# The first pair of gate and up: computed from h block by block instead of by seven products, with the factors of h on VectorE alone

## The chip, the cores and the metric

One core of a Trainium2 chip runs the whole program. The time is device microseconds of one launch: before, 2615.62 us as the median of three runs (2615.2 to 2616.56). A profiled execution of the same program took 2614.02 us, of which 2612.3 us lie between its first and its last instruction (its span).

## What is computed

The reference is one layer of a hybrid decoder for 1024 prompt tokens and 64 sample tokens (8 groups of 8), so 1088 token columns, with a model width of 1024. The layer is a half feed-forward, an attention and Mamba mixer with an output projection, a second half feed-forward and a final norm. The change is in the two feed-forwards:

```python
def rmsnorm(x, w):
    xf = x.astype(jnp.float32)
    y = xf * lax.rsqrt(jnp.mean(xf * xf, axis=-1, keepdims=True) + EPS)
    return (y * w.astype(jnp.float32)).astype(x.dtype)

def ffn_half(x, nw, wg, wu, wd):
    h = rmsnorm(x, nw)
    return x + 0.5 * ((jax.nn.silu(h @ wg) * (h @ wu)) @ wd)
```

wg and wu are 1024 x 2816: 22 blocks of 128 feature rows, handled as 11 pairs.

## The kernel before

**Number format.** All products are float32 in value. Each operand is split into a high part, rounded to the TensorE format fp32r, and a low part, the rest (`split`: a cast on ScalarE, VectorE or GpSimd, and a subtraction). A product then takes three matmuls: high x high, low x high, high x low.

**Seven products.** h, transposed, stands as eight blocks of 128 model features by 1088 tokens. It is seen as a 2 x 2 matrix: features 0 to 511 (blocks kk = 0..3) and 512 to 1023 (blocks kk + 4), by token half (544 columns each): h11, h21 are the two feature halves of the first token half, h12, h22 those of the second. A pair of 128-row blocks of a weight, with its two feature halves, is a 2 x 2 matrix too. The 2 x 2 product is made by seven products instead of eight (Winograd's form). It needs seven factors B1..B7 of h (h11, h21, h22, h12-h11, h22-h12 and two longer sums) and seven factors of each weight pair, every one as a high and a low tile. The factors of h are made once per feed-forward (`b_make`) and used by 11 pairs of gate and 11 of up; the factors of a weight (`factors`) are made for each pair. The token halves are worked in two column parts, `SUBS`: 256 columns (part 0), then 288 (part 1) of each half. A product is 4 x 3 matmuls (k = 0..3) with a moving operand of 256 or 288 columns, so one pair of one weight has 7 x 12 x 2 = 168 of them, and `Product.product` then adds each into the result tile `Cc` on ScalarE or VectorE (lines 358 to 372).

**The first pair (p = 0) of a feed-forward** runs while the factors of h come into being, since nothing else can run then. In the first feed-forward `x_sub(z)` makes part z of h: sums of squares on ScalarE (`x_rms`, line 591), transposes on TensorE into PSUM (line 607), the normed value h on VectorE (line 609), a copy of the raw value to DRAM by ScalarE (line 610), and `b_make` for each block kk. `begin1` then orders: seven products of gate on part 0, part 1 of h, seven of up on part 0, and, with the weight factors made a second time, gate and up on part 1. In the second feed-forward `begin2` does the same; part 0 of its factors (`b0`) is made between the output projection's last products (`out`, lines 1877 to 1886), and part 1 after the norm of the layer's x (`x2_sq`, `x2_rms`, `h_row`). Which engine does each subtraction and cast of these first factors is written in the strings CFG1, CFG2 and BC: v is VectorE, p GpSimd, a ScalarE.

```python
CFG1 = [('pvppvppvppv', 'vvvvavv'), ('pvppvvvppvv', 'aaaaaaa'), ...
BC = [('vvpvvppvppv', 'vvvvvvv'), ('pvpvvppvvpv', 'vvaaaaa'), ...
```

**Pairs p = 1..10** use `Product` with subtractions on VectorE and casts on ScalarE. While pair p runs, `g_factors` splits the result of pair p - 1 for the down projection and writes it to DRAM (GD).

**What sets the order.** The program is written once; a scheduler that estimates the time of each instruction lays it out as one fixed queue per engine, and a queue waits at its first instruction that is not ready. Tiles come from pools: a new tile of a tag waits for one of the tag's buffers to come free (for `Cc` three, for the PSUM tags X and Y four banks each).

Of the kernel before, what the change touches and what calls it, by code (L numbers as in the profile page):

```python
# [82 lines left out]
def hybrid_step(ctx: ExitStack, tc: tile.TileContext, *aps):  # L83
# [34 lines left out]
    F1X, F1R, F1, F1W, F1T = (F1s.enter_context(pool(nm, bufs=2)) for nm in ("f1x", "f1r", "f1c", "f1w", "f1t"))  # L118
# [7 lines left out]
    for tag, bufs in (("h0", 2), ("h1", 2), ("h2", 1), ("h3", 1), ("t0", 1), ("t1", 1), ("xRs", 2)):  # L126
        FX.first(tag, [P, 288], bufs)
# [22 lines left out]
    raw0 = F1R.tile([P, 8, 2 * P], F32, name="raw", tag="raw", bufs=2)  # L150
# [1978 lines left out]
```

## Time and profile before

| quantity | before |
|---|---|
| median of the runs | 2615.62 us |
| profiled execution, its span | 2614.02 us, 2612.3 us |
| TensorE (PE) busy | 2465.2 us, 94% of the span |
| VectorE (DVE) busy | 1863.4 us, 71% |
| ScalarE (ACT) busy | 1103.0 us, 42% |
| GpSimd (POOL) busy | 642.9 us, 25% |
| last up result of pair 0, first feed-forward | added at 120.81 us |
| last up result of pair 0, second feed-forward | added at 1938.72 us |

Rows of the timeline read: start, length, engine, line, operation, result<-operands, shape, and in brackets how long the engine was idle before and who ended it. Instructions overlap at their ends by some 0.07 us on VectorE and by more on TensorE, so the time that one takes from its queue is read from start to start. Rows of windows read: busy time (and count) of PE, PE's weight loads, DVE, ACT and POOL, the granted PE clock, the share of the DMA engines, GB/s.

### The profile page before, as it was taken

The numbers are of one execution on the slowest core, as the hardware profiler recorded it, in microseconds if no ns is written. First come the engines' busy times: TensorE is split into PE (matmuls) and PEld (weight loads), VectorE is DVE, ScalarE is ACT, GpSimd is POOL, SyncE is SP. The second block draws the span as 40 slices with busy tenths as digits, with TensorE's granted clock in tenths as the row PEclk, the third lists the DMA queues.
The fourth block names the chain that finished last, engine by engine and source line by source line (L and its number), as shares of the span: only waits on it lengthen the run. The fifth ranks groups of instructions, "written<-read, shape, count | busy, mean of one in ns | idle before, by whom it ended". The sixth has DMA issues, their size and how long they took to land.

```text
span 2612.3 us, 47418 instructions
## 1 busy us (share of the span) xinstructions
PE 2465.2 (94%) x18647; PEld 2291.2 (88%) x18647; DVE 1863.4 (71%) x3699; ACT 1103.0 (42%) x2410; POOL 642.9 (25%) x703
## 2 busy tenths in 40 slices
PE   5899999999999999999999979999689999999998
PEld 4799999999999999878787756678689999999998
DVE  7967676776677556377778877567986766768666
ACT  4544444431233223277777633423244544442113
POOL 5500000013234223444344345232620000002220
PEclk9899999999999999999999989989889999999999
DMA  4243443496553222220101134352123434469653
GB/s 138 83 164 134 149 153 127 167 385 256 198 193 104 88 60 90 89 82 33 65 34 36 54 130 162 120 180 95 54 99 123 164 128 160 150 230 349 234 185 146
DMA packets 209531, 365.05 MB, mean 140 GB/s; under 512 B 17053, under 2 KB 130377, under 8 KB 207388
## 3 DMA queue, kind: packets, MB, share of 16 engines
q1 hardware_dynamic: 190376, 305.10, 33.6%
q0 software_dynamic: 7600, 38.59, 4.1%
q10 hardware_dynamic: 11332, 18.33, 2.0%
q8 instruction: 147, 2.41, 0.4%
q14 instruction: 76, 0.62, 0.1%
HBM read 246.39 MB, written 119.71 MB: 140 GB/s over the span
## 4 chain that ended last, share of the span: by engine, by line
PE 45%; DVE 9%; DMA 3%; ACT 2%; issue 1%; POOL 0%; SPq 0%; DVEq 0%; ACTq 0%; POOLq 0%
PE gY L353 3%; PE gY L352 3%; PE gY L354 3%; PE dq L551 3%; PE dq L552 3%; PE dq L553 3%; PE gX L353 2%; PE gX L354 2%; PE gX L352 2%; PE pT L1521 2%; PE o L1526 1%; PE o L1527 1%; PE s L1484 1%; PE cA L1397 1%; PE s_ps L1743 1%
## 5 line engine op out<-in xcount | busy, mean ns | idle before, releaser
L552 PE MATMUL dq<-db,da 128*128 128x256 f32 (+1 forms) x1232 | 354.7, 290 | 3.1 <-DVE da L258 2.9
L553 PE MATMUL dq<-db,da 128*128 128x256 f32 (+1 forms) x1232 | 354.2, 289 | 0.0
L551 PE MATMUL dq<-db,da 128*128 128x256 f32 (+1 forms) x1232 | 349.2, 290 | 5.1 <-DMA db<-GD 3.3
L557 DVE TENSOR_TENSOR xT<-xT,dq 128x256 f32<-128x256 f32 (+1 forms) x520 | 210.1, 431 | 118.5 <-PE dq L553 117.3
L258 POOL TENSOR_TENSOR ds<-dw 128x512 f32<-128x512 f32 x22 | 29.1, 1323 | 1033.3 <-PE gY L353 423.1
L552 PEld LDWEIGHTS dq<-db,da 128*128 128x128 f32 x1232 | 233.4, 190 | 4.5 <-DVE da L258 4.3
L551 PEld LDWEIGHTS dq<-db,da 128*128 128x128 f32 x1232 | 230.4, 190 | 6.5 <-ACT da L255 2.4
L553 PEld LDWEIGHTS dq<-db,da 128*128 128x128 f32 x1232 | 234.0, 190 | 0.0
L255 ACT CAST whi<-ws 128x512 fp32r<-128x512 f32 x178 | 110.4, 623 | 219.0 <-PE gY L354 155.5
L255 ACT CAST da<-ds 128x512 fp32r<-128x512 f32 x88 | 51.9, 619 | 254.0 <-PE dq L553 91.5
L258 DVE TENSOR_TENSOR wlo<-raw,whi 128x512 fp32r<-128x512 f32 x149 | 109.0, 737 | 70.3 <-ACT whi L255 69.9
L258 DVE TENSOR_TENSOR wlo<-ws,whi 128x512 fp32r<-128x512 f32 x175 | 124.6, 715 | 47.3 <-ACT whi L255 46.5
L255 ACT CAST whi<-raw 128x512 fp32r<-128x512 f32 x158 | 98.0, 626 | 77.3 <-DMA raw<-in_w_out_dram 49.0
L1500 ACT ACTIVATE pb<-s,mx 128x256 f32<-128x256 f32 (+3 forms) x192 | 105.4, 555 | 36.0 <-DVE mx L1498 17.2
L258 DVE TENSOR_TENSOR pl<-pT,ph 128x512 fp32r<-128x512 f32 (+1 forms) x148 | 100.1, 683 | 20.8 <-ACT ph L255 19.5
L352 PE MATMUL gY<-B3h,whi 128*128 128x256 f32 (+1 forms) x352 | 101.8, 290 | 6.1 <-DVE Cc L368 5.4
L353 PE MATMUL gY<-B5h,wlo 128*128 128x256 f32 (+1 forms) x352 | 101.9, 290 | 4.8 <-DVE wlo L258 4.7
L352 PE MATMUL gX<-B6h,whi 128*128 128x256 f32 (+1 forms) x352 | 103.5, 294 | 2.8 <-ACT Cc L359 2.5
L353 PE MATMUL gY<-B4h,wlo 128*128 128x256 f32 (+1 forms) x352 | 101.9, 292 | 3.7 <-DVE wlo L258 3.7
L352 PE MATMUL gY<-B4h,whi 128*128 128x256 f32 (+1 forms) x352 | 99.8, 291 | 5.2 <-DVE whi L255 3.2
L255 ACT CAST ph<-pT 128x512 fp32r<-128x512 f32 (+1 forms) x148 | 84.8, 588 | 46.4 <-PE pT L1521 44.4
L352 PE MATMUL gX<-B1h,whi 128*128 128x256 f32 (+1 forms) x352 | 100.8, 293 | 3.2 <-DVE whi L255 2.4
(683 smaller groups left out, 8853.3 us busy)
## 6 DMA issues: line engine op xcount, KB each, us to landing
db<-GD SPq DMA_DIRECT2D x42, 1632.0 KB
GD<-Cc SPq DMA_DIRECT2D x154, 272.0 KB
GD<-his SPq DMA_DIRECT2D x84, 272.0 KB
raw<-in_ffn_wg_dram SPq DMA_DIRECT2D x22, 1024.0 KB
raw<-in_ffn_wu_dram SPq DMA_DIRECT2D x22, 1024.0 KB
dw<-in_ffn_wd_dram SPq DMA_DIRECT2D x44, 512.0 KB
GD<-hp SPq DMA_DIRECT2D x70, 272.0 KB
db<-GD SPq DMA_DIRECT2D x14, 1088.0 KB
```

Of the source, the lines that this page charges most:

```text
L255: nc.scalar.copy(out, src) if eng == "a" else ENGINES[eng].tensor_copy(out, src)
L258: ENGINES[eng].tensor_tensor(out, x, y, op=op)
L352: nc.tensor.matmul(q, ah[:, k], b_, start=first, stop=False, skip_group_check=True)
L353: nc.tensor.matmul(q, al[:, k], b_, start=False, stop=False, skip_group_check=True)
L354: nc.tensor.matmul(q, ah[:, k], c_, start=False, stop=(k == 3), skip_group_check=True)
L551: nc.tensor.matmul(q, x, bh[:, u, o], start=first, stop=False, skip_group_check=True)
L552: nc.tensor.matmul(q, y, bh[:, u, o], start=False, stop=False, skip_group_check=True)
L553: nc.tensor.matmul(q, x, bl[:, u, o], start=False, stop=(u == np_ - 1), skip_group_check=True)
L557: nc.vector.tensor_tensor(x, x, q, op=OP.subtract if i == 4 else OP.add)
L1397: nc.tensor.matmul(ab, wh, mh, start=first, stop=False, skip_group_check=True)
L1500: nc.scalar.activation(pb[:, st:st + pn], s, AF.Exp, bias=mx[:, 0:1], accum_out=part[:, hh_, i:i + 1])
L1521: nc.tensor.transpose(tq_[:kn, P * hh_:P * hh_ + P], src, ident)
```

## The change

For p = 0 alone the seven products are replaced by the plain eight. Class `First` takes the four blocks of h as they are (B1 = h11, B4 = h12 for now, B2 = h21, B3 = h22) and two feature blocks of the raw weight (kk and kk + 4, 256 columns), splits them in one 128 x 512 piece, and accumulates all of a column part in PSUM: per kk 2 x 2 x 2 x 3 = 24 matmuls, as soon as block kk of h is there. Gate leaves PSUM through SiLU on ScalarE, up through one multiplication on VectorE (`silu_out`, `times_out`); the additions into `Cc` and the sums of weight blocks fall away for this pair. `b_make` first splits the four plain blocks, then makes the differences; the sum that belongs in B4 is kept in a tile T4, and `b_last` writes it over h12 once First has read it. All subtractions of these factors are on VectorE, all casts on ScalarE; CFG1, CFG2 and BC are gone. In the second feed-forward T4 and three of the h rows take two of the three `Cc` buffers for a while, and "hp" has five buffers instead of four.

```diff
-    def b_make(K, h, kk, z, eng="vvpvvppvppv", heng="vvaaaaa"):
+    def b_make(z, kk, h):
...
         def put(i, src):
-            split(BN[z][i][0][:, kk], BN[z][i][1][:, kk], src, next(e), next(he))
+            split(BN[z][i][0][:, kk], BN[z][i][1][:, kk], src, "v")
         put(1, h11)
         put(2, h21)
...
+        put(4, h12)
+        put(3, h22)
+        sub("v", h11, h12, h11)
+        sub("v", h12, h22, h12)
+        sub("v", h22, h22, h11)
+        sub("v", t4, h22, h21)
+        put(6, h22)
         put(7, h12)
-        put(5, t1)
-        put(3, h22)
-        sub(next(e), h21, t2, h21)
-        put(4, h21)
+        put(5, h11)
+
+    def b_last(z):
+        for kk in (0, 2):
+            split(*(t[:, kk:kk + 2] for t in (*BN[z][4], T4[z])), "v")
...
+    class First:
...
+        def run(self, z, kk, bank):
+            c0, n = SUBS[z]
+            src = self.raw[:, kk::4]
+            hi, lo = (F1W.tile([P, 2, 2 * P], F32R, name=f"w{c}", tag=f"w{c}", bufs=4) for c in ("hi", "lo"))
+            split(hi, lo, src, "v")
+            if kk == 0:
+                if z == 0:
+                    t = [bank("g0") for _ in range(2)]
+                    self.q = {(f, j): t[f][:, n * j:n * j + n] for f in range(2) for j in range(2)}
+                else:
+                    self.q = {(f, j): bank("g0")[:, :n] for f in range(2) for j in range(2)}
+            for i in range(2):
+                for j in range(2):
+                    bh, bl = (t[:, kk] for t in BN[z][((1, 4), (2, 3))[i][j]])
+                    for f in range(2):
...
+                        nc.tensor.matmul(q, hi[:, i, o], bh, start=first, stop=False, skip_group_check=True)
+                        nc.tensor.matmul(q, lo[:, i, o], bh, start=False, stop=False, skip_group_check=True)
+                        nc.tensor.matmul(q, hi[:, i, o], bl, start=False, stop=last, skip_group_check=True)
+            if kk == 3:
+                for f in range(2):
+                    for j in range(2):
+                        self.out(self, f, slice(HALF * j + c0, HALF * j + c0 + n), self.q[f, j])
+
+    def silu_out(g, f, o, q):
+        nc.scalar.activation(g.C[:, f, o], q, AF.Silu)
...
-    def begin1(g, u):
-        for i in ORDER:
-            g.product(i, 0)
-        x_sub(1)
-        for i in ORDER:
-            u.product(i, 0)
-        for x, c in ((g, CFG1[2]), (u, CFG1[3])):
-            x.begin(*c)
-            for i in ORDER:
-                x.product(i, 1)
+    def begin1():
+        g = First(F1, w1g, silu_out, raw0)
+        x_sub(0, lambda kk: g.run(0, kk, bankx))
+        u = First(F1, w1u, times_out(g))
+        for kk in range(4):
+            u.run(0, kk, bankx)
+        x_sub(1, lambda kk: g.run(1, kk, bankx))
+        b_last(0)
+        for kk in range(4):
+            u.run(1, kk, banky)
+        b_last(1)
+        return [g, u]
```

**Place 1: VectorE in the first feed-forward, a block of part 1.** Names: h_* are normed blocks, B1h/B1l the high and low tile of factor 1, t_* differences, ws sums of weight blocks, wlo low parts of weights. Before, VectorE's queue has there:

```order
L609 SCALAR_TENSOR_TENSOR h_643<-x_ps,w_170,xRs 128x288
L609 SCALAR_TENSOR_TENSOR h_650<-x_ps,w_170,xRs 128x288
L258 TENSOR_TENSOR B3l_77<-h_614,B3h_76 128x288
L258 TENSOR_TENSOR wlo<-ws_851,whi 128x512
L258 TENSOR_TENSOR B5l_84<-t_618,B5h_83 128x288
L255 CAST B1h_111<-h_643 128x288
L370 TENSOR_TENSOR Cc<-Cc,gY 128x256
L258 TENSOR_TENSOR B6l_98<-t_619,B6h_97 128x288
```

and GpSimd's beside it, before:

```order
L258 TENSOR_TENSOR h_598<-t_619,h_598 128x288
L258 TENSOR_TENSOR B7l_91<-h_607,B7h_90 128x288
L258 TENSOR_TENSOR ws_889<-raw,ws_831 128x512
L258 TENSOR_TENSOR wlo<-ws_830,whi 128x512
L258 TENSOR_TENSOR B1l_112<-h_643,B1h_111 128x288
L258 TENSOR_TENSOR t_670<-h_659,h_643 128x288
```

Now VectorE has:

```order
L641 SCALAR_TENSOR_TENSOR h_771<-x_ps,w_168,xRs 128x288
L257 TENSOR_TENSOR B4l_70<-h_705,B4h_69 128x288
L641 SCALAR_TENSOR_TENSOR h_778<-x_ps,w_168,xRs 128x288
L257 TENSOR_TENSOR B3l_77<-h_712,B3h_76 128x288
L257 TENSOR_TENSOR h_705<-h_712,h_705 128x288
L257 TENSOR_TENSOR B5l_84<-h_689,B5h_83 128x288
L257 TENSOR_TENSOR B1l_112<-h_771,B1h_111 128x288
L257 TENSOR_TENSOR h_712<-h_712,h_689 128x288
L257 TENSOR_TENSOR B2l_105<-h_778,B2h_104 128x288
```

GpSimd's queue has no instruction in this feed-forward's first pair any more; VectorE has all subtractions, no casts, and no sums of weights.

**Place 2: TensorE in the first feed-forward, the change from part 0 to part 1.** Before, the transposes of part 1 (x_ps) stand in the middle of the products of part 0:

```order
L354 MATMUL gX<-B6l_96,whi 128x256
L352 MATMUL gY<-B4h_67,whi 128x256
L607 MATMUL x_ps<-ident,xt 128x128 x2
L607 MATMUL x_ps<-ident,xrest 128x32
L607 MATMUL x_ps<-ident,xt 128x128 x2
L607 MATMUL x_ps<-ident,xrest 128x32
L352 MATMUL gX<-B7h_88,whi 128x256
```

Now (g_519 and g_520 are up's sums on part 0; xR spreads the norm of part 1):

```order
L398 MATMUL g_520<-B3h_74,wlo 128x256
L399 MATMUL g_520<-B3l_75,whi 128x256
L216 MATMUL xR<-ident,xr_634 128x128 x2
L216 MATMUL xR<-ident,xr_634 128x32
L216 MATMUL xR<-ident,xr_659 128x128
L216 MATMUL xR<-ident,xr_659 128x96
L216 MATMUL xR<-ident,xr_659 128x64
L639 MATMUL x_ps<-ident,xt 128x128 x2
L639 MATMUL x_ps<-ident,xrest 128x32
```

The norm and the transposes of part 1 moved behind all of gate's and up's products on part 0.

**Place 3: the second feed-forward.** Before, TensorE has products of gate on part 0 between the two steps of part 1's norm (nps sums, nR spreads):

```order
L354 MATMUL gY<-B2l_20727,whi 128x256
L743 MATMUL nps<-ones,acc 128x1 x4
L743 MATMUL nps<-ones,acc 64x1
L352 MATMUL gY<-B5h_20741,whi 128x256
L353 MATMUL gY<-B5h_20741,wlo 128x256
L354 MATMUL gY<-B5l_20742,whi 128x256
```

Now all of them stand behind the norm:

```order
L239 MATMUL wout<-ol,whi 128x288
L781 MATMUL nps<-ones,acc 128x1 x4
L781 MATMUL nps<-ones,acc 64x1
L216 MATMUL nR<-ident,nr 128x128 x4
L791 MATMUL nps<-ident,nr 128x64
L397 MATMUL g_21456<-B1h_20663,whi 128x256
```

And VectorE now has, at the end of the factors of part 1 (hpc: h rows in a `Cc` buffer; g_21649 and g_21650: up's sums on part 0; L410 is `times_out`):

```order
L257 TENSOR_TENSOR T_20704<-hpc 128x288
L257 TENSOR_TENSOR B6l_21422<-hpc,B6h_21421 128x288
L257 TENSOR_TENSOR wlo<-raw,whi 128x512
L410 SCALAR_TENSOR_TENSOR Cc<-Cc,g_21649 128x256 x2
L410 SCALAR_TENSOR_TENSOR Cc<-Cc,g_21650 128x256 x2
L257 TENSOR_TENSOR ws_22097<-raw 128x512
L257 TENSOR_TENSOR ws_22141<-raw 128x512
L257 TENSOR_TENSOR ws_22098<-ws_22097,raw 128x512
L257 TENSOR_TENSOR wlo<-raw,whi 128x512 x5
```

`times_out` of part 0 stands behind the last use of hpc, and frees the PSUM banks that gate's second half of part 1 takes; the first sums of the next pair's weight (ws) stand ahead of the low parts of up's weight for part 1 (wlo).

More of the change, by code (lines that the diff above doesn't have):

```diff
@@ L149, in hybrid_step @@
         x_load(t0, n)
-    raw0 = F1R.tile([P, 8, 2 * P], F32, name="raw", tag="raw", bufs=2)
+    raw0 = f32(F1R.tile([P, 8, 2 * P], F32R, name="raw", tag="raw", bufs=2))
     nc.sync.dma_start(raw0, A["ffn1_wg"][0][:, :2 * P].rearrange("(k p) f -> p k f", p=P))
@@ L429, in gate_up @@
                         up(int(i == 4))
-            elif p == 0:
-                ps.append(Product(K, wu, p, 1, cfg=cfg[1]))
-                begin(*ps)
-                for f in range(2):
-                    gate(f)
-                    up(f)
-            else:
+            elif p:
                 for x in every:
@@ L455, in gate_up @@
             pass
-    raws, loaded = {}, []
+    loaded = []
     def gu_raw(K, w, p):
-        raw = F1R.tile([P, 8, 2 * P], F32, name="raw", tag="raw", bufs=2)
+        raw = f32(F1R.tile([P, 8, 2 * P], F32R, name="raw", tag="raw", bufs=2))
         load = nc.sync.dma_start(raw, w[:, 2 * P * p:2 * P * p + 2 * P].rearrange("(k p) f -> p k f", p=P))
@@ L622, in x_sub @@
             x_block(s, kk)
+            product(kk)
     def late():
@@ L1920, in hybrid_step @@
     FX = Ahead(F1X)
-    FX.first("hp", [P, 576], 4)
-    for tag in ("t0", "t1"):
-        FX.first(tag, [P, 288])
+    FX.first("hp", [P, 576], 5)
     FX.first("acc", [P, 576], 2)
@@ L1958, in h_row, with h_of @@
         return h
+    def h_of(x, y):
+        n = x.shape[-1] // 2
+        return x[:, :n], y[:, :n], x[:, n:], y[:, n:]
+    t4 = F1.tile([P, 4, HALF], F32, name="T4", tag="Cc", bufs=3)
+    T4[0], T4[1] = t4[:, :, :256], t4[:, :, 256:]
     for m in range(KD):
@@ L1977, in hybrid_step @@
     x2_rms(1)
[L1978 to L1981 removed]
+    hp = [FX.tile("hp", [P, 576], 5) for _ in range(5)]
+    c = F1.tile([P, 2, T], F32, name="hpc", tag="Cc", bufs=3).rearrange("p a t -> p (a t)")
+    hp += [c[:, 576 * u:576 * u + 576] for u in range(3)]
     rows = {m: h_row(m, 1, hp.pop(0)) for kk in range(4) for m in (kk, kk + 4)}
@@ L1996, in banky, with begin2 @@
         return PY.tile([P, 512], F32, name=name, tag="Y", bufs=4)
-    def begin2(g, u):
-        for i in ORDER:
-            g.product(i, 0)
+    def begin2():
+        g = First(F1, A["ffn2_wg"][0], silu_out)
         for kk in range(4):
-            b_make(FX, h_of(rows[kk], rows[kk + 4]), kk, 1, *BC[3])
-        for i in ORDER:
-            u.product(i, 0)
-        for x, c in ((g, CFG2[2]), (u, CFG2[3])):
-            x.begin(*c)
-            for i in ORDER:
-                x.product(i, 1)
-    gate_up(F1, A["ffn2_wg"][0], A["ffn2_wu"][0], begin2, CFG2, lambda: FX.tile("hp", [P, HALF], 4, F32R),
-            lambda: [FX.tile("hp", [P, 4, P], 4) for _ in range(3)])
+            g.run(0, kk, bankx)
+        for kk in range(4):
+            b_make(1, kk, h_of(rows[kk], rows[kk + 4]))
+        u = First(F1, A["ffn2_wu"][0], times_out(g))
+        for kk in range(4):
+            u.run(0, kk, bankx)
+        b_last(0)
+        for kk in range(4):
+            g.run(1, kk, bankx)
+        for kk in range(4):
+            u.run(1, kk, banky)
+        b_last(1)
+        return [g, u]
+    gate_up(F1, A["ffn2_wg"][0], A["ffn2_wu"][0], begin2(), lambda: FX.tile("hp", [P, HALF], 5, F32R),
+            lambda: [FX.tile("hp", [P, 4, P], 5) for _ in range(3)])
     R2s.close()
```

75 lines of the change are left out of this document (35 added, 40 removed).

## The prediction

> **What bounds the kernel now.** I read the page's span, then the busy time of each engine in stretches of the two feed-forwards, then the timeline's rows in them, and the groups by shape.
>
> ```profile
> span 2612.3 us, 47418 instructions
> ```
>
> The windows give start:end, length, then the busy time (and count) of TensorE (PE), its weight loads, VectorE (DVE), ScalarE (ACT), GpSimd (POOL), the granted clock, the DMA share and GB/s:
>
> ```profile
> 11.00:56.00 45.00, 24.98 (x97) 19.78 (x98) 43.70 (x88) 16.84 (x53) 29.72 (x30) 0.94 0.37 120
> 56.00:118.40 62.40, 52.62 (x332) 46.43 (x332) 56.26 (x92) 32.41 (x74) 37.67 (x32) 0.85 0.20 62
> 118.40:140.00 21.60, 21.60 (x175) 21.60 (x174) 19.09 (x33) 12.00 (x23) 0.00 (x0) 1.00 0.67 230
> ...
> 1811.00:1860.00 49.00, 41.50 (x288) 39.08 (x286) 48.30 (x78) 13.65 (x28) 35.20 (x33) 0.97 0.27 85
> 1860.00:1902.00 42.00, 24.38 (x140) 22.16 (x140) 38.51 (x59) 13.25 (x32) 23.66 (x21) 0.74 0.08 27
> 1902.00:1936.00 34.00, 30.47 (x203) 29.16 (x204) 27.64 (x42) 15.74 (x30) 12.37 (x9) 0.87 0.15 46
> 1936.00:2100.00 164.00, 164.00 (x1329) 164.00 (x1328) 118.06 (x203) 77.90 (x155) 0.00 (x0) 1.00 0.45 151
> ```
>
> From 118.4 and from 1936 on PE has no gap: 21.60 of 21.60 us and 164.00 of 164.00. In the first pair of the first feed-forward (11 to 118.4) it has 77.6 of 107.4 us, while DVE has 100.0 and POOL 67.4; in the second (1811 to 1936) PE has 96.4 of 125, DVE 114.5. So **DVE's list of factors bounds the first pairs, PE all that follows**, and what a first pair gains passes to the end 1:1. Its end on PE:
>
> ```profile
> 118.56 0.38 ACT L359 COPY Cc<-gX 128x256 f32<-128x256 f32 x1 [0.92 <-PE gX L354]
> ...
> 120.81 0.46 DVE L370 TENSOR_TENSOR Cc<-Cc,gY 128x288 f32<-128x288 f32 x1 [1.24 <-PE gY L354]
> ...
> 1938.72 0.46 DVE L370 TENSOR_TENSOR Cc<-Cc,gY 128x288 f32<-128x288 f32 x1 [1.25 <-PE gY L354]
> ```
>
> DVE adds up's last product of pair 0 at 120.81; at 118.56 a product of pair 1 was already copied out, so by the queue some 18 matmuls had run ahead: 18 x 0.13 = 2.3 us, and the pair's work equals an end at 118.4. In the same way 1938.72 stands for 1936.3.
>
> DVE's busy time is stretched. Two groups of one shape, the one beside POOL, the other mostly without it:
>
> ```profile
> L258 DVE TENSOR_TENSOR B6l<-t,B6h 128x288 fp32r<-128x288 f32 x4 | 4.3, 1066 | 0.0
> ...
> L258 DVE TENSOR_TENSOR t<-h,t 128x288 f32<-128x288 f32 x4 | 1.8, 448 | 0.0
> ```
>
> 1066 ns against 448. The rows that stand alone, read from start to start:
>
> ```profile
> 19.52 0.41 DVE L258 TENSOR_TENSOR B1l<-h,B1h 128x256 fp32r<-128x256 f32 x1
> 19.85 0.41 DVE L258 TENSOR_TENSOR B2l<-h,B2h 128x256 fp32r<-128x256 f32 x1
> ...
> 70.90 1.35 DVE L609 SCALAR_TENSOR_TENSOR h<-x_ps,w,xRs 128x288 f32<-128x288 f32 x3
> ...
> 115.13 0.68 DVE L258 TENSOR_TENSOR ws<-raw 128x512 f32<-128x512 f32 x1
> 115.73 0.68 DVE L258 TENSOR_TENSOR wlo<-raw,whi 128x512 fp32r<-128x512 f32 x1
> ...
> 1905.13 0.45 DVE L258 TENSOR_TENSOR B5l<-t,B5h 128x288 fp32r<-128x288 f32 x1
> 1905.50 0.44 DVE L258 TENSOR_TENSOR hpc<-t,hpc 128x288 f32<-128x288 f32 x1
> ```
>
> **Prices.** A subtraction of 256 columns goes by 0.33 (19.52 to 19.85), of 288 by 0.37, of 512 by 0.60; three h rows of 288 by 0.43 each. The h row of 256, read from PSUM, I put between those at 0.39, a 576-wide one at 0.65. PE and ACT:
>
> ```profile
> 20.93 0.41 PE L352 MATMUL gX<-B1h,whi 128*128 128x256 f32 x1
> 21.14 0.41 PE L353 MATMUL gX<-B1h,wlo 128*128 128x256 f32 x1
> ...
> 39.14 0.58 PE L352 MATMUL gX<-B1h,whi 128*128 128x256 f32 x1 [0.40 <-DVE B1h L255]
> ...
> 47.00 0.30 PE L353 MATMUL gY<-B5h,wlo 128*128 128x256 f32 x1
> ...
> 62.39 0.28 PE L354 MATMUL gX<-B1l,whi 128*128 128x256 f32 x1
> 62.50 0.28 PE L352 MATMUL gX<-B1h,whi 128*128 128x256 f32 x1
> ...
> 63.18 0.38 PE L607 MATMUL x_ps<-ident,xt 128*128 128x128 f32 x2
> ...
> 63.67 0.44 PE L607 MATMUL x_ps<-ident,xt 128*128 128x128 f32 x2
> ...
> 115.63 0.29 PE L352 MATMUL gY<-B4h,whi 128*128 128x288 f32 x1
> 115.76 0.30 PE L353 MATMUL gY<-B4h,wlo 128*128 128x288 f32 x1
> ```
>
> ```profile
> 18.65 0.58 ACT L591 ACTIVATE xsq<-xt 128x512 f32<-128x512 f32 x1
> ...
> 65.41 0.45 ACT L255 CAST B7h<-h 128x288 fp32r<-128x288 f32 x1
> ...
> 105.70 1.28 ACT L413 ACT_TABLE_LOAD   x1
> ...
> L413 ACT ACTIVATE Cc<-Cc x44: 1097/1111/1117, 107.0 to 2353.2; 128x1088 f32<-128x1088 f32 x44
> ```
>
> A matmul of 256 columns has a pitch of 0.115 (62.39, 62.50) or, at half rate, 0.21 (20.93, 21.14); of 288 it has 0.13 (115.63). After an idle stretch PE worked from 39.14 to about 47.00 at the slow pitch before the fast one came, 7.8 us, so a cold start costs some 3.5 us.
>
> The Trainium skill ("TensorE: Matmul & The Clock Gate", Part 1 on the clock gate) says that the array runs at half clock for about 3.4 us of activity and falls back after an idle window. The two pitches agree, the 7.8 us do not; by the page's 3.4 each cold start would cost about 1.7 us, an estimate, and the sum below would be some 5 us lower.
>
> **What goes and what comes.** The plain eight need 4 x 24 = 96 matmuls per weight and column part, 384 per feed-forward, where seven products needed 336: 48 more, 48 x 0.123 = 5.9 us of PE. Gone are the first pair's additions into Cc, the sums of weight blocks, the second making of weight factors, and all of POOL's part. DVE's list in the first feed-forward is now 16 h rows and 4 outputs of up (L609-like, one operand in PSUM) of each width, 44 subtractions of each width, 16 weight low parts and 2 pieces of B4 of 512, 2 of 576: 20 x 0.39 + 20 x 0.43 + 44 x 0.33 + 44 x 0.37 + 18 x 0.60 + 2 x 0.65 + 1 = **60 us** where 100.0 were busy. If the stretch were not POOL's, the same list at 0.8 to 1.0 an instruction would take some 100 us and nothing would be won on DVE. ACT gets all casts: 56 of h (0.34, row 65.41) and 20 of weights or B4 (0.6, as the 512-wide square), 32 raw copies (0.37), 20 squares (0.6, row 18.65) and 8 SiLUs, about 58 us. SiLU from PSUM is in no row; the nearest below is the copy Cc<-gX, 0.38, above it a whole SiLU of 1088 columns (1.11 for the last row's group); I take 0.4, near the copy, whose width it has. At 1.11 the eight would cost ACT 6 us more ahead of part 1. Up's outputs lie between the 0.37 and 0.46 of rows above. The table loads for SiLU and the root cost 1.28 each (105.70).
>
> **First feed-forward.** The first h row stood at 14.30, that of part 1 at 55.78:
>
> ```profile
> 14.30 0.86 DVE L609 SCALAR_TENSOR_TENSOR h<-x_ps,w,xRs 128x256 f32<-128x256 f32 x2
> ...
> 55.78 0.93 DVE L609 SCALAR_TENSOR_TENSOR h<-x_ps,w,xRs 128x288 f32<-128x288 f32 x2
> ```
>
> Now four gate low parts (4 x 0.60) precede h: start at 16. Part 0 then needs of DVE 16 x 0.39 + 44 x 0.33 + 4 x 0.60 = 23.2, to about 40; of PE 192 x 0.115 = 22, transposes 5 (16 groups without the remainder), a cold start 3.5, and it is fed block by block: I put its end at 50 (bounds 46.5, the bare sum from 16, and 58, a wait of 3 for each of four blocks). The norm of part 1 moves behind part 0 on PE (transposes) and behind SiLU on ACT (queue order): from gate's end near 44, two table loads 2.6, SiLUs 1.6, ten squares 6, root, spread and copies 2: first h at 57, PE idle about 5. Part 1 from there: PE 192 x 0.13 = 25, transposes 8.6 (16 groups of 0.49, rows 63.18 and 63.67, and the spread of the norm), cold start 3.5, so 37; DVE 16 x 0.43 + 44 x 0.37 + 8 x 0.60 = 28 lies beside it. End 94, with 2 for waits **96, a gain of 22** from 118.4. Bounds: 88.6 when the handover costs 4 instead of 7 and neither start is cold (gain 30), 105 when part 0 ends at 58 (gain 13).
>
> **Second feed-forward.**
>
> ```profile
> 1859.49 0.44 DVE L1886 TENSOR_TENSOR xT<-xT,wout 128x288 f32<-128x288 f32 x1
> ...
> 1867.64 3.86 DVE L1956 SCALAR_TENSOR_TENSOR hp<-xT,vec,acc 128x576 f32<-128x576 f32 x4 [0.84 <-ACT acc L755]
> ...
> 1921.36 0.37 SPq L461 DMA_DIRECT2D raw<-in_ffn_wg_dram  x1
> ...
> 1929.95 1.74 DVE L258 TENSOR_TENSOR ws<-raw 128x512 f32<-128x512 f32 x1
> ```
>
> The output projection's last add is at 1859.49; there PE was idle 7.5 of 49 us while DVE (48.30 of 49) made part 0's factors with POOL's 35.2 beside it. The new DVE list in this stretch is 16 x 0.39 + 44 x 0.33 for factors and about 16 for the projection, 37: end at 1852 (bounds 1848, PE without idle and 4 more for what it also shed, and 1860, nothing won). The norm takes 8.15 from there to the h rows (1859.49 to 1867.64) and gate's products now stand behind it: 1858 + 22 + 3.5 = 1883.5. Meanwhile DVE does the 8 h rows of 576 (0.74, twice 0.37; at most 0.97, 3.86 / 4), 44 x 0.37, 8 x 0.60 and 1.2 of B4: from 1860 to 1888.5. Only then come up's outputs, since u.C waits for the tile of the h rows; the PSUM banks of gate's part 1 wait for them, so **a new wait of about 5 us** stands on PE ahead of gate's second half, with all of gate and up part 1 behind it: 1889 + 192 x 0.13 = **1914, a gain of 22** from 1936.3. The next pair's ws<-raw stands ahead of five low parts on DVE; its load went out at 1921.36 and its tile was read by 1929.95, so at most 8.6 us; issued now near 1886.5 it lands by 1895, needed at 1899: covered by some 4 us, beyond which each microsecond late costs one. Bounds: 1901 (projection 1848, no cold start, half the wait), gain 35; 1926 (projection 1860, the rest as above, 4 more wait), gain 10.
>
> **Sum.** 22 + 22 = 44. The profiled execution took 2614.0 us, the median of the runs 1.6 more: 2615.6 - 44 = **2571.5 us**. The bounds (23 to 65) give 2550 to 2592.
>
> **Rivals.**
> 1. *Half pitch in the block-by-block parts.* PE is fed in pieces there, and rows 20.93 to 47.00 show half pitch under such feeding; against it, gaps become shorter than before. Part 0 at 192 x 0.21 = 40 instead of 22 + 3.5: the first pair ends near 111, the second's at 1928, gains 7 and 8: 2600. The skill's rule on the clock (same page and part) falls in with this if every window has idle time.
> 2. *The handovers of the queues swallow half.* DVE, ACT and PE each hold some 60 us in order; against it, ACT was the least busy of the three (16.84 of 45 and 32.41 of 62.40 us), so its new load has room. If only one feed-forward gains, 2615.6 - 22 = 2593.
> 3. *Better.* No cold start and no wait at the handovers: 2550.
> 4. *Slower.* PE stays at half pitch in both column parts of both feed-forwards: 192 x (0.21 + 0.24) = 86 us of matmuls per feed-forward. First: 16 + 40 + 4 to 60, 7 of handover, 46 and transposes at half pitch to 134 (loses 16); second: 1858 + 40 + 46 and the wait of 5 to 1949 (loses 13): 2644. It decides once more than 44 / 0.11 = 400 of the 768 matmuls run so. Against it: rows 62.39 to 62.50 already have the full pitch in part 1 before.
> 5. *It does not do what it says*: the stretch of DVE stays though POOL is idle, and PE's 2 x 5.9 us come on top: 2627. Row pairs such as 1066 against 448 speak against it.
>
> **How the numbers follow.** Forecast 0.62, rival 1 0.10, rival 2 0.14, rival 3 0.06, rival 4 0.05, rival 5 0.03. The range takes the forecast's bounds, widened to most of rivals 1 to 3: 2546 to 2602; the likeliest case by itself has 2550 to 2592. This measurement tells 0.2%, some 5 us, from no change. Faster: 0.62 + 0.10 + 0.14 + 0.06 less 0.01 for their edges, 0.91; within 0.2%: 0.02; slower 0.07.
>
> **What would show it.** Right: DVE's subtractions of 256 and 288 columns at means of 0.41 and 0.45 with POOL empty in 11 to 100; first h of part 1 at 57; the pair's end at 96; in the second feed-forward an idle PE of some 5 us ahead of gate's second half, ended by up's output; from the pairs' ends on a PE without gaps. Wrong: a pitch of 0.21 in most of part 0, DVE means near 0.8, or PE idle in the later pairs (a load or factor late there), which would cost beside all of this.

## The result, and the profile after

| quantity | before | after |
|---|---|---|
| median of the runs | 2616.09 us (4 runs, 2615.2 to 2616.96) | 2573.79 us (4 runs, 2572.59 to 2577.71) |
| ratio of the medians, 95% interval | | 0.9841, 0.9824 to 0.9858 |
| profiled execution, its span | 2614.02, 2612.3 us | 2574.34, 2572.6 us |
| GpSimd busy | 642.9 us | 508.1 us |
| VectorE busy | 1863.4 us | 1781.9 us |

The changed kernel is 42.3 us faster by the medians, 39.7 by the profiled executions; the forecast was 2571.5. The stretches of the changed kernel, in the form of the windows of before (start:end, length, then busy us and count of PE, its weight loads, DVE, ACT, POOL, then the granted clock, DMA share, GB/s):

```profile
11.00:50.00 39.00, 32.39 (x234) 30.50 (x234) 30.16 (x79) 31.06 (x89) 0.00 (x0) 1.00 0.43 138
50.00:57.00 7.00, 2.84 (x11) 2.18 (x11) 2.03 (x6) 4.13 (x9) 0.00 (x0) 0.62 0.44 148
57.00:96.00 39.00, 38.58 (x221) 33.07 (x220) 30.09 (x74) 22.19 (x56) 0.00 (x0) 0.81 0.27 84
...
1811.00:1850.00 39.00, 34.62 (x236) 33.65 (x235) 33.18 (x69) 18.84 (x42) 4.09 (x3) 0.87 0.40 130
1850.00:1875.00 25.00, 25.00 (x208) 25.00 (x207) 23.41 (x58) 15.56 (x37) 0.00 (x0) 1.00 0.07 21
1875.00:1900.00 25.00, 25.00 (x195) 25.00 (x194) 14.82 (x26) 10.54 (x19) 0.00 (x0) 1.00 0.27 89
...
1936.00:2100.00 164.00, 164.00 (x1331) 164.00 (x1330) 117.29 (x203) 76.84 (x155) 0.00 (x0) 1.00 0.43 148
```

POOL is empty in the first pair of the first feed-forward, DVE went from 100.0 busy us to about 63, and PE's largest hole is at 50 to 57. In the windows from 1850 on PE has no gap. The trace has no record of the clock ahead of its first change (20.99 here), and the windows print 1.00 there. The groups of VectorE's subtractions in 11 to 98 (last columns: busy us, mean ns of one, idle before):

```profile
L257 DVE TENSOR_TENSOR h<-h,h 128x288 f32<-128x288 f32 x12 | 5.4, 453 | 0.0
L257 DVE TENSOR_TENSOR h<-h,h 128x256 f32<-128x256 f32 x12 | 5.0, 420 | 0.1
L257 DVE TENSOR_TENSOR B6l<-h,B6h 128x288 fp32r<-128x288 f32 x4 | 1.8, 453 | 0.0
```

The low part of B6, which took 1066 ns beside POOL, takes 453. The marks on which the working stood, in the timeline after (in brackets how long the engine had been idle, and who ended it):

```profile
16.58 1.80 DVE L641 SCALAR_TENSOR_TENSOR h<-x_ps,w,xRs 128x256 f32<-128x256 f32 x4 [1.74 <-PE x_ps L639]
...
54.16 1.75 PE L216 MATMUL xR<-ident,xr 128*128 128x128 f32 x6 [4.54 <-DVE xr L214]
...
56.81 0.52 DVE L641 SCALAR_TENSOR_TENSOR h<-x_ps,w,xRs 128x288 f32<-128x288 f32 x1 [2.80 <-PE x_ps L639]
...
98.31 0.28 PE L351 MATMUL gX<-B1h,whi 128*128 128x256 f32 x1
...
1834.88 0.45 DVE L1924 TENSOR_TENSOR xT<-xT,wout 128x288 f32<-128x288 f32 x1
...
1843.69 0.58 PE L397 MATMUL g<-B1h,whi 128*128 128x256 f32 x1
...
1868.08 0.30 PE L398 MATMUL g<-B1h,wlo 128*128 128x288 f32 x1
...
1872.01 1.40 DVE L410 SCALAR_TENSOR_TENSOR Cc<-Cc,g 128x256 f32<-128x256 f32 x4
...
1874.32 0.29 PE L397 MATMUL g<-B4h,whi 128*128 128x288 f32 x1
...
1893.42 0.28 PE L351 MATMUL gX<-B1h,whi 128*128 128x256 f32 x1
```

The pairs p = 1 begin on PE at 98.31 and 1893.42, where before the equivalents were 118.4 and 1936.3. So the first feed-forward gained 20.1, and up to the second pair's end the program gained 42.9. The difference, 22.8, is not what the second feed-forward gained, for the lead of the first did not arrive there whole. Three like rows, first before, then after (the same SiLU of a later pair in each feed-forward, and between them the reciprocal in the norm that is taken during the output projection):

```profile
182.13 1.11 ACT L413 ACTIVATE Cc<-Cc 128x1088 f32<-128x1088 f32 x1
1806.34 0.18 DVE L215 RECIPROCAL nr<-nr 128x4 f32<-128x4 f32 x1 [0.27 <-ACT nr L214]
1999.62 1.11 ACT L413 ACTIVATE Cc<-Cc 128x1088 f32<-128x1088 f32 x1
```

```profile
162.84 1.11 ACT L452 ACTIVATE Cc<-Cc 128x1088 f32<-128x1088 f32 x1
1793.05 0.18 DVE L214 RECIPROCAL nr<-nr 128x4 f32<-128x4 f32 x1 [0.27 <-ACT nr L213]
1956.71 1.11 ACT L452 ACTIVATE Cc<-Cc 128x1088 f32<-128x1088 f32 x1
```

The lead is 19.3 us at the first, 13.3 at the second and 42.9 at the third: 6.0 us were lost between the feed-forwards, and the second one gained 29.6. Most of the loss lies from 1715 to 1775, where PE has the output projection among its work and waits for a weight's high part, 1.51 us before and 4.53 after:

```profile
1765.81 0.49 PE L238 MATMUL wout<-oh,whi 128*128 128x512 f32 x1 [1.51 <-ACT whi L255]
```

```profile
1751.61 0.79 PE L237 MATMUL wout<-oh,whi 128*128 128x512 f32 x1 [4.53 <-ACT whi L254]
```

In that stretch PE, DVE, ACT and POOL have the same instructions in the same order before and after, but for one matmul. The loss mostly goes with the time that the clock is at half between the first pair's end and 1790: 81.9 us before, 92.2 after. Of the runs below, three with 99.0 us there lost 8.4 of their lead on the way (the two mixed ones and the order of loads alone), two with 81.9 lost 1.2 and 1.6, and one with 75.1 (the third that fills the hole) lost nothing; but the early norm lost only 2.8 with 92.2. What causes the loss is not shown.

From the second pair's end to the end of the span it took 2572.6 - 1893.4 = 679.2 instead of 676.0: **3.2 us were given back**, at a place that the prediction had not looked at. 19.3 - 6.0 + 29.6 - 3.2 is the 39.7 of the profiled executions. The rows of TensorE's waits in the last 280 us, before and after (total us, times, longest):

```profile
PE dq L551 <- DMA db<-GD: 2.1, 1, 2.1
```

```profile
PE dq L584 <- DMA db<-GD: 8.5, 3, 4.9
```

It is the last down projection, whose products wait for their operands (db). SyncE's queue there, before and after (SPq: the issue of DMAs):

```profile
2335.11 5.74 SPq L698 DMA_DIRECT2D xT<-xD  x2
2342.22 7.88 SPq L504 DMA_DIRECT2D db<-GD  x3
```

```profile
2297.10 0.38 SPq L537 DMA_DIRECT2D db<-GD  x1
2297.53 0.93 SPq L736 DMA_DIRECT2D xT<-xD  x2
2300.17 4.56 SPq L537 DMA_DIRECT2D db<-GD  x2
```

The scheduler laid this queue in another order, though nothing of the change is there: one db now stands ahead of the two loads of x and holds them. Down's first product started at 2355.47 before, 20 us behind the first issue of x, and at 2310.09 after, 12.6 us behind it.

### The profile page after: what moved, and what is told of

Same layout as the page of the kernel before. It is cut to its first block, busy times and chain, and to the rows that moved or that the text cites. A ratio compares the mean times of both kernels' runs of the same rounds, so it can differ in the third digit from the quotient of the medians.

```text
span 2572.6 us, 47482 instructions
## 1 busy us (share of the span) xinstructions
PE 2459.7 (96%) x18743; PEld 2293.1 (89%) x18743; DVE 1781.9 (69%) x3677; ACT 1114.6 (43%) x2452; POOL 508.1 (20%) x581
## 4 chain that ended last, share of the span: by engine, by line
PE 46%; DVE 6%; DMA 4%; ACT 2%; issue 2%; POOL 1%; SPq 0%; DVEq 0%; ACTq 0%; POOLq 0%
PE gY L352 3%; PE gY L351 3%; PE gY L353 3%; PE dq L584 3%; PE dq L586 3%; PE dq L585 3%; PE gX L351 2%; PE gX L352 2%; PE gX L353 2%; PE pT L1559 2%; DMA db<-GD 1%; PE o L1565 1%; PE o L1564 1%; PE s L1522 1%; DMA chk<-in_cache_cmp_dram,idx 1%
## 5 line engine op out<-in xcount | busy, mean ns | idle before, releaser
L254 ACT CAST whi<-ws 128x512 fp32r<-128x512 f32 x156 | 96.4, 622 | 210.7 <-PE gY L353 142.2
L254 ACT CAST whi<-raw 128x512 fp32r<-128x512 f32 x176 | 108.9, 625 | 91.2 <-DMA raw<-in_w_out_dram 48.3
L257 DVE TENSOR_TENSOR wlo<-ws,whi 128x512 fp32r<-128x512 f32 x156 | 106.9, 689 | 41.5 <-ACT whi L254 41.0
L1535 DVE TENSOR_REDUCE mx<-s 128x1 f32<-128x384 f32 (+2 forms) x128 | 67.5, 536 | 38.6 <-PE s L1527 30.2
L264 POOL TENSOR_TENSOR pb<-pb,sm 128x640 f32<-128x640 f32 (+7 forms) x70 | 84.9, 1236 | 44.1 <-DVE sm L1545 43.6
L351 PE MATMUL gY<-B3h,whi 128*128 128x256 f32 (+1 forms) x320 | 91.5, 287 | 1.4 <-ACT whi L254 1.4
L352 PE MATMUL gX<-B6h,wlo 128*128 128x256 f32 (+1 forms) x320 | 91.8, 287 | 0.5 <-DVE wlo L257 0.5
L351 PE MATMUL gX<-B6h,whi 128*128 128x256 f32 (+1 forms) x320 | 91.4, 286 | 0.7 <-ACT Cc L358 0.7
L352 PE MATMUL gY<-B3h,wlo 128*128 128x256 f32 (+1 forms) x320 | 91.7, 287 | 0.2 <-DVE wlo L257 0.2
```

The source lines that it names most:

```text
L254: nc.scalar.copy(out, src) if eng == "a" else ENGINES[eng].tensor_copy(out, src)
L257: ENGINES[eng].tensor_tensor(out, x, y, op=op)
L264: nc.gpsimd.tensor_tensor(out, x, by.to_broadcast(list(x.shape)), op=OP.mult)
L351: nc.tensor.matmul(q, ah[:, k], b_, start=first, stop=False, skip_group_check=True)
L352: nc.tensor.matmul(q, al[:, k], b_, start=False, stop=False, skip_group_check=True)
L1535: nc.vector.tensor_reduce(mx[:, 1 + i:2 + i], parts[i][0], axis=AX.X, op=OP.max)
```

## Experiments: what the gain consists of

The theory was that GpSimd's subtractions stretch VectorE's, and that block-by-block products shorten the list on top; the rivals were that only the one or only the other counts, or that only one feed-forward pays.

**The kernel before with all subtractions on VectorE.**

```diff
-CFG1 = [('pvppvppvppv', 'vvvvavv'), ('pvppvvvppvv', 'aaaaaaa'), ...
+CFG1 = [('vvvvvvvvvvv', 'aaaaaaa')] * 4
+CFG2 = CFG1
+BC = CFG1
```

> The kernel before, with its seven products, but every subtraction of the first pairs' factors on VectorE and every cast on ScalarE: only GpSimd's share is undone. Theory (GpSimd's subtractions stretch VectorE's, and the plain eight products shorten its list): VectorE's list in the first feed-forward becomes 32 h rows (13 us), 88 subtractions of h (31), four sets of 11 weight subtractions at 0.6 (26) and 16 additions at 0.4 (6), some 78 us instead of 100 busy, so about half the gain: 2585 to 2602. Rival 1 (the stretch is not GpSimd's, only the form of the products matters): VectorE gets more to do, 2616 or slower. Rival 2 (all of the gain is GpSimd's absence): about 2574.

Measured: 2584.21 us, ratio 0.9874 (0.9858 to 0.9891). That is just under the expected band, and more than the expected half of the gain. Its windows and one group:

```profile
11.00:56.00 45.00, 30.51 (x152) 25.39 (x153) 37.93 (x99) 33.46 (x100) 0.00 (x0) 0.96 0.39 126
56.00:98.00 42.00, 35.90 (x236) 31.79 (x237) 38.80 (x88) 29.17 (x67) 0.00 (x0) 0.88 0.24 78
...
L258 DVE TENSOR_TENSOR B6l<-t,B6h 128x288 fp32r<-128x288 f32 x4 | 1.8, 454 | 0.0
```

VectorE has all subtractions of two engines and is busy 76.7 us to 98 and 81.8 to the pair's end at 103.1, where it was busy 100.0 before. But the same edit also moves all casts to ScalarE. Before, VectorE's casts in 11 to 118.4 were these (windows of the cast's line alone: DVE, ACT and POOL, then clock and DMA):

```profile
11.00:118.40 107.40, 22.02 (x44) 21.47 (x43) 0.00 (x0) 0.89 0.27 86
```

Without them VectorE was busy 78.0 us with 94 of the subtractions beside GpSimd's 62; the 81.8 are for all 156. So some three quarters of the gain, 31.7 to 31.9 us by the medians, come from this division of the list: no subtraction on GpSimd, and no cast on VectorE, where 44 casts took 22.0 us. The run does not part the two, and none was made with the casts left on VectorE; the next two runs show GpSimd's share by itself. The plain eight products bring the other 10. In the trace the pair ends, by the same rows as before, at 103.1 and 1907.1: against the changed kernel the form of the products is worth 4.8 us at the first pair's end (no more than the clock's chance moves it, see below) and 13.7 at the second's, of which the 3.2 at the last down projection are lost again (this kernel has no wait for db at all). At the reciprocal near 1806 this kernel leads the one before by 14.1 us, the changed kernel by 13.3: of the 4.8 nothing is left there, so the 13.7 are gained in the second feed-forward.

**The changed kernel with part of the list back on GpSimd.**

```diff
-        put(2, h21)
+        put(2, h21, "p")
...
-        put(3, h22)
+        put(3, h22, "p")
...
-        sub("v", t4, h22, h21)
+        sub("p", t4, h22, h21)
...
-        put(7, h12)
-        put(5, h11)
+        put(7, h12, "p")
+        put(5, h11, "p")
```

> The changed kernel, with 5 of the 11 subtractions of each block of h (low parts of B2, B3, B5, B7 and the sum T4) put back on GpSimd in both feed-forwards. Theory: VectorE loses 40 instructions of 0.35 (14 us) per feed-forward, but its others stretch to 0.8 or more beside GpSimd's, which take 1.0 to 1.2 each and are waited for by the products: 10 to 25 us slower, 2584 to 2599. Rival (two engines share the list, no contention): 2565 to 2574.

Measured: 2587.89 us, ratio 0.9901 (0.9882 to 0.992), 14 us slower than the changed kernel. Groups of VectorE and GpSimd in 11 to 98:

```profile
L257 DVE TENSOR_TENSOR h<-h,h 128x288 f32<-128x288 f32 x12 | 9.1, 759 | 0.7 <-POOL B3l L257 0.5
...
L257 POOL TENSOR_TENSOR B3l<-h,B3h 128x288 fp32r<-128x288 f32 x4 | 4.2, 1048 | 6.0 <-DVE h L641 3.3 <-ACT B3h L254 2.7
```

Forty subtractions fewer, and VectorE is still busy 60.6 of these 87 us where the changed kernel has 63.0, since others stretched: the differences of 288 columns from 453 to 759 ns. Only 1.6 us of the loss are in the first feed-forward (pair 1's first copy at 101.49 instead of 99.92, both with 20.5 us at half clock); by the second one's pair 1 it is 12.9 (1907.89 instead of 1895.00).

**GpSimd working beside, on nothing.** Nine subtractions on a tile of its own are added per block of h in the first feed-forward:

```diff
+        for _ in range(9 if beside else 0):
+            nc.gpsimd.tensor_tensor(beside[0], beside[0], beside[0], op=OP.subtract)
```

> The changed kernel, with 9 subtractions of 256 columns on a tile of their own added on GpSimd for each block of h of the first feed-forward (72 in all); nothing depends on them, and VectorE's list is as it was. Theory (contention between the two engines): VectorE's subtractions of 256 and 288 columns there rise from 0.42 to 0.8 or more, the first pair ends 10 to 30 us later than 98.3, total 2584 to 2604. Rival (no contention): within 2 us of 2574.

Measured: 2583.47 us, ratio 0.9872 (0.9855 to 0.9888); the first pair ends 11.1 us later (first copy of pair 1 at 111.05).

```profile
L257 DVE TENSOR_TENSOR h<-h,h 128x256 f32<-128x256 f32 x12 | 9.0, 746 | 0.1
...
L257 DVE TENSOR_TENSOR B4l<-h,B4h 128x288 fp32r<-128x288 f32 x4 | 1.8, 454 | 0.0
...
L297 POOL TENSOR_TENSOR beside<-beside 128x256 f32<-128x256 f32 x59 | 41.4, 702 | 4.6
```

A row of GpSimd's timeline in the same run gives its pitch:

```profile
19.83 20.82 POOL L297 TENSOR_TENSOR beside<-beside 128x256 f32<-128x256 f32 x28
```

59 of the 72 fall into 11 to 98. VectorE's list and its data are as in the changed kernel; where GpSimd runs (part 0, 256 columns) the mean is 746 instead of 420 ns, and where it has finished (part 1, 288 columns) it is 454. That is contention between the two engines and nothing else; the total is a little under the expected band, and GpSimd was done at 56.9, before part 1. GpSimd's 28 subtractions take 20.82 us, 0.744 each, the same as VectorE's mean of 0.746: the two look as if they took turns. The h rows, which read one operand from PSUM, stay at 0.471 to 0.515 in every run. The Trainium skill ("SBUF — State Buffer", "SBUF: two separate sides") states that a VectorE operation with two inputs in SBUF and a GpSimd operation that reads SBUF exclude each other for the whole instruction; these rows agree with it, in which operations stretch and in the equal pitch.

**The change in the first feed-forward alone.** The second keeps `begin2`, CFG2 and BC of before.

> The change in the first feed-forward alone; the second has the seven products with its factors shared with GpSimd as before. Theory (the two gains, about 20 and 23 us on TensorE, are independent and pass through unshortened): 2616 - 20 = 2596, at most 3 us off. Rival (only one of the two pays, or the first pays back later): 2574 or 2616.

Measured: 2594.76 us, ratio 0.9915 (0.9898 to 0.9931): 21.2 of the 42.3 us (18 to 27 by the interval). Both feed-forwards pay, about half each by the medians. Its trace is of its slowest execution (2602.14 us), with 27.3 us at half clock in the first pair (below), and keeps only 12 us to the end, so the traces can't confirm the halves.

## Experiments: what the first feed-forward still loses

PE's hole at 50 to 57 is followed by a long stretch at half clock. Two rows of windows of the changed kernel at its two ends:

```profile
52.00:54.00 2.00, 0.00 (x0) 0.00 (x0) 0.86 (x2) 1.77 (x3) 0.00 (x0) 0.50 0.06 15
...
72.00:74.00 2.00, 2.00 (x12) 1.26 (x11) 0.33 (x1) 0.76 (x2) 0.00 (x0) 0.95 0.80 279
```

The clock falls to 0.50 before 54 and comes back only behind 72, though PE is busy from 54.16 on; in the second feed-forward full pitch came 3.4 us after gate's first product. The question was whether the gap or the transposes between the products do it.

**The norm's statistics early.** The squares, root and reciprocal of part 1 are taken between the blocks of part 0:

```diff
             x_block(s, kk)
             product(kk)
+            if s == 0 and kk in (1, 2):
+                x_stat(SUBS[1][0] + HALF * (kk - 1))
```

> The changed kernel with the squares, root and reciprocal of part 1 of the first feed-forward placed between the blocks of part 0; only the spreading matmuls and the h rows remain behind it, and the two extra table loads go. Theory (TensorE's 4.5 us ahead of part 1 are ScalarE's list: SiLU, squares, table loads): the first h of part 1 comes at about 52 instead of 56.8, 2568 to 2571. Rival (ScalarE's 6 us of squares delay the casts of part 0, so nothing is won): 2573 to 2577.

Measured: 2563.42 us, ratio 0.9801 (0.9783 to 0.982), **10 us faster than the changed kernel**, more than expected.

```profile
50.00:57.00 7.00, 7.00 (x53) 5.95 (x51) 4.34 (x9) 4.19 (x10) 0.00 (x0) 1.00 0.10 26
...
54.01 1.06 DVE L654 SCALAR_TENSOR_TENSOR h<-x_ps,w,xRs 128x288 f32<-128x288 f32 x2 [0.58 <-PE x_ps L652]
...
68.87 0.40 PE L397 MATMUL g<-B4h,whi 128*128 128x288 f32 x1 [2.00 <-DVE Cc L410]
```

The hole at 50 to 57 is gone and h comes 2.8 us earlier; the clock stays at 1.00 until up's outputs on VectorE (L410), which free PSUM banks, make PE wait 2.00 at 68.87. Then it is at half for 3.4 us, as it was once before, at 25.1; the changed kernel had 20.5. ScalarE's list was the cause of the hole. The transposes still stand between the products, from 53 to 66, and without the hole ahead of them the clock did not fall there, here and in the second run with the early norm. Not all of the 10 us can be put down to the edit: in the trace pair 1's first copy stands at 94.09, 5.8 earlier than in the changed kernel's trace, and 4.8 more arise from there to pair 1 of the second feed-forward (1884.41 against 1895.00), where the edit changes nothing.

**Filling the hole.** Matmuls into a bank that nobody reads, or transposes, behind up's part 0; for this B4's rewriting was put ahead of part 1 in the program:

```diff
+        b_last(0)
+        fill(30)
         x_sub(1, lambda kk: g.run(1, kk, bankx))
-        b_last(0)
```

> The changed kernel with 30 matmuls (256 columns, into a PSUM bank that nobody reads) in TensorE's gap between up's part 0 and the norm of part 1 of the first feed-forward; they start when the last low part of B4 is there (50.6) and should fill the 3.6 us to 54.2. B4's rewriting stands ahead of part 1 in the program. Theory 1 (what keeps TensorE at half pitch until 73 are the transposes between the products, not the gap ahead of them): part 1 goes back to half pitch while its first transposes run; 2571 to 2575. Theory 2 (only the gap ahead counts): the 17 us at half pitch become full pitch, 8 us less, 2564 to 2568.

> The same with 14 transposes of 128 columns in that gap instead of the matmuls. Theory 1: half pitch as in the changed kernel, 2572 to 2577. Theory 2 in the form that any work of TensorE counts: 2564 to 2568, as the matmuls. If matmuls help there and transposes don't, transposes don't count as work for the clock.

> The same 30 matmuls in the gap, and 4 more behind each of the first 8 groups of transposes of part 1 (32 x 0.115 = 3.7 us of TensorE at full pitch). Theory 1: the products never drop to half pitch, 8.5 us won, 3.7 spent: about 2569. Rival (VectorE's h rows and ScalarE set the pace of part 1, the clock does not): 2574 to 2579.

Measured: 2577.42 (0.986, 0.9833 to 0.9886), 2583.62 (0.9878, 0.9856 to 0.99) and 2569.31 us (0.9827, 0.9808 to 0.9846). They don't tell the theories apart: the shifted rewriting delayed the second half of the norm, which is not what was meant to change. In all three the first pair ends later than in the changed kernel (pair 1's first copy at 101.78, 109.06 and 105.72, not 99.92), so the third's 2569, though forecast, did not come about as it was forecast.

```profile
60.10 1.76 PE L216 MATMUL xR<-ident,xr 128*128 128x128 f32 x6 [3.75 <-DVE xr L214]
```

This is the run with the matmuls: the spread of the norm's second half stands at 60.10, not 54.16, and the clock falls at 56.0 anyway, between a gap of 2.37 us and this one of 3.75.

**Transposes among products, without a gap.** In the second feed-forward two matmuls (control), or two transposes, were pinned behind each 6 products of part 0:

```diff
+                    if mixed and z == 0:
+                        t = banky("mix")
+                        with tc.issue_after(at.ins):
+                            for _ in range(2):
+                                nc.tensor.transpose(t[:, :128], ident, ident)
```

> The changed kernel, with 2 matmuls of 128 columns (into a bank that nobody reads) behind each 6 products of gate's and up's part 0 in the second feed-forward, 64 in all, pinned to that place. It is the control of the next run. Both theories: TensorE starts at half pitch as in the changed kernel and reaches full pitch after about 3.4 us; 64 x 0.06 to 0.11 = 4 to 7 us more, 2577 to 2582.

> The same with 2 transposes of 128 columns in place of the 2 matmuls, at the same 32 places; here no other wait lies between the products. Theory 1 (transposes between products hold TensorE at half pitch, as in part 1 of the first feed-forward): products at 0.21 for 10 us or more after 1843.7, 2590 to 2602. Theory 2 (the half pitch of the first feed-forward came from waits or from the gap ahead): full pitch after 3.4 us, 64 x 0.16 to 0.18 = 11 us more, 2583 to 2588.

Measured: 2582.75 us (0.9871, 0.9855 to 0.9888) for the matmuls, a little above the band, and 2577.4 us (0.9845, 0.9827 to 0.9863) for the transposes, which is under both bands forecast for them. The profiled executions don't show why: they took 2579.67 and 2579.92 us, with pair 1's first copy of the second feed-forward at 1900.22 and 1900.01. The windows of the run with transposes:

```profile
1842.00:1844.00 2.00, 2.00 (x11) 2.00 (x11) 2.00 (x4) 0.97 (x3) 0.00 (x0) 0.50 0.00 0
1844.00:1846.00 2.00, 2.00 (x13) 2.00 (x13) 2.00 (x4) 1.20 (x3) 0.00 (x0) 0.63 0.00 0
1846.00:1848.00 2.00, 2.00 (x20) 2.00 (x19) 2.00 (x5) 1.39 (x4) 0.00 (x0) 1.00 0.00 0
```

The clock is back at the same place as in the control, whose row from 1844 to 1846 has 0.51: 4.1 us after gate's first product here, 4.3 there. Theory 1, that any transposes between products hold the half clock, falls in this dose. In the first feed-forward the dose is larger (from 54 to 60 there are only transposes, then a group of them behind 2 to 6 products), and chance comes in: in the changed kernel, in the kernel with the first feed-forward alone and in three others (the two mixed ones and the one below) PE, ACT and DVE have the same instructions in the same order there, and yet the time at 0.50 between 48 and 88, summed from windows of 1 us, was 20.5, 27.3, and three times 10.2 us. All are whole multiples of 3.41: 6, 8 and 3. A row of one of the latter, with the DMA order changed far behind:

```profile
62.00:64.00 2.00, 2.00 (x10) 1.65 (x9) 2.00 (x6) 1.17 (x3) 0.00 (x0) 0.57 0.10 8
```

There the clock is back at 64, with the same instructions that left it at half until 72 in the changed kernel. Pair 1's first copy came at 96.14 with 3 such windows, at 99.92 with 6, and at 102.87 with 8, 1.3 to 1.5 us for each. The Trainium skill ("TensorE: Matmul & The Clock Gate", Part 1 on the clock gate) says that the window is about 3.4 us long and runs freely, and that one busy window releases the clock; the multiples of 3.41 agree with its length, and the different counts in equal code with its running freely. That one busy window is enough does not show: from 54.16 to 72.19 in the changed kernel, five windows long, PE's row has 18.03 busy of 18.03 us, products and transposes, at 0.50. How much of a window must be products is not settled by these runs.

## Experiments: what was given back at the end

**The order of SyncE's queue.** The first db is issued behind the loads of x, as before the change:

```diff
+            for z in range(2):
+                load = nc.sync.dma_start(xT.tiles[z], xD[:, 4 * z:4 * z + 4])
+            with tc.issue_after(load.ins):
+                for z in range(2):
+                    D2.fetch(z)
```

> The changed kernel, with the first load of products (db) of the last down projection put behind the two loads of x (xT) in SP's queue, where it stood in the kernel before; all else as it is. Theory (the 3 us that the change loses between the second feed-forward's first pair and the end come from that order: xT's 4.4 MB go out 9 us later and share the DMA with the second and third db): TensorE's 8.5 us of waiting for db there shrink to 2 to 4, total 2567 to 2571. Rival (the bytes are the same and as late in any order, or the loss is elsewhere): 2573 to 2577.

> Both together: the statistics of part 1's norm early, and db behind xT in SP's queue. Theory: the two add, 2563.4 - 5 = 2557 to 2561. Rival (as for the run on the order): 2562 to 2566.

Measured: 2565.88 us, ratio 0.9806 (0.9792 to 0.9821), and with the early norm 2564.11 us, 0.9794 (0.9779 to 0.981). TensorE's waits in the last down projection of the first of the two:

```profile
PE dq L584 <- issue: 2.2, 1, 2.2
PE dq L584 <- ACT da L254: 1.7, 1, 1.7
PE dq L584 <- DVE xT L590: 1.3, 1, 1.3
```

The waits for db are gone; 5.2 us of others stand in their place. From pair 1's start to the end it takes 2567.5 - (1892.15 - 1.58) = 676.9 us (1892.15 is its first copy, 1.58 the distance from the start to that copy in the changed kernel), so the order brought back 2.3 of the 3.2 us. The other traces bear that out: from that first copy to the end it took 676.5 to 679.2 us in the nine with the changed second feed-forward and db ahead, 675.4 and 675.6 in the two with db behind. The profiled executions differ by 5.1 us in all (2574.34 and 2569.21); 3.8 are the three windows fewer at half clock in the first pair, which are chance, 2.3 the order, and 0.9 is lost between. The median fell by more, 7.9 us, which the traces don't explain, so 2.3 is what may be put down to the order. Together with the early norm the median (2564.11) is not below that of the early norm alone (2563.42), although in the trace the last part is as short (675.6 us from the first copy, 679.1 with the early norm alone); other stretches took 3 us longer. The two ratios, 0.9794 and 0.9801, don't part them either. Whether the two add is open.

## Why the prediction was right, point by point

- **What bounds**: right in the first pairs. "What a first pair gains passes to the end 1:1" is the first step that failed. It was read from two windows without a gap, 118.4 to 140 and 1936 to 2100; of the first pair's lead of 19.3 us 13.3 were left at the second feed-forward, and 3.2 of the whole went at the last down projection.
- **VectorE's prices**: right to a few ns. 0.33 and 0.37 from start to start (means 420 and 453), h rows of 0.43, the eight 576-wide rows 1843.92 to 1849.8, 0.74 each as taken. Rival 5 falls.
- **First feed-forward, part 0**: h at 16.58 (16 was said), part 0 done by 49 (50 was said). The slow pitch of 0.21 lasted only from gate's first product at 17.90 to 21, some ten products or 1 us, where 3.5 were charged; before it had lasted to 47.00.
- **Handover**: h at 56.81 (57 was said), PE idle 4.54 (5 was said) for the reason given, the norm behind ScalarE's list. Taking that list away removed it.
- **Part 1** is the first mis-sized term: 41.5 us from 56.8 to 98.3, where 39 were allowed (37 and 2 for waits). The "cold start 3.5" was 20.5 us at half clock, which at 1.3 a window costs about 8. Rival 1's mechanism was thus there in part, in part 1 rather than part 0, and it is chance how long it lasts: with 3 windows the copy of pair 1 came 3.8 us earlier, with 8 it came 3.0 later, so that the 22 were met within 2 is in part luck. The Trainium skill's window is the unit, but the number of windows was not one.
- **Second feed-forward, the output projection**: the last add at 1834.88 is 24.6 earlier, 13.3 of it inherited, so 11.3 against 7.5 forecast (1859.5 to 1852), near the bound that was given (1848).
- **Second feed-forward, the "new wait of about 5 us"** is the other step that failed: VectorE's timing was right (up's outputs at 1872.01, 3.9 us after PE was done with part 0 at 1868.08), but PE did not wait. The queue has the products of gate's first token half ahead (1868.08 to 1874.2), in the two banks that SiLU had freed, and only at 1874.32 those that need up's banks. With the cold start at 3.4 us of half clock (1.7 lost, not 3.5) and the shorter projection this made the gain of this feed-forward 29.6, where 22 was said.
- **Not foreseen**: the queue of SyncE 400 us behind the change, 3.2 us.

The sum of the pairs' ends, 42.9, was forecast as 44, but that is in part luck: by the like rows the errors are -2.7 in the first pair (19.3 for 22), -6.0 on the way to the second, +7.6 in the second (29.6 for 22) and -3.2 at the end, and the two largest nearly cancel. Two bounds don't come out of their terms: 88.6 would be 86 (96 less 3, 3.5 and 3.5), and 1901 would be 1904 (1914 less 4, 3.5 and 2.5); the range hardly moves. What the prediction did not do is to split the gain: it priced the two changes together, and the runs show the new division of the list (GpSimd out, casts to ScalarE) at about 32 us and the form of the products at about 10.

## What to carry to other kernels

Read the mean of one shape with and without the neighbour engine at work before sharing a list between VectorE and GpSimd: here VectorE alone needed hardly longer for all subtractions (82 us) than for its share of them beside GpSimd (78), and these settings, which also moved the casts to ScalarE, gave three quarters of the gain. When products are made to start earlier, look at what now stands between two batches of them on the engine that feeds them: moving the norm's statistics ahead brought as much by the medians as the new form of the products, a good half of it in the first pair itself. Follow a lead through the whole program by like rows of the two traces before adding up the gains of two places: 6 of 19 us were lost on the way here. A change that alters instruction counts can move DMAs in a queue far away, so compare the queues to the end of the program.

## What was not expected of the hardware

The half clock came in multiples of 3.41 us, 3, 6 or 8 of them with equal instructions on PE, ACT and DVE, and moved the end of the first pair by 6.7 us (96.14 to 102.87) from one profiled execution to another. A single trace's difference below that, in a kernel with an idle TensorE followed by transposes and products, shows nothing about an edit.
